# Rows of log decays from a table and one product per tile, and the gates ahead of the features, in a hybrid DeltaNet and attention step

## Chip, cores and metric

One core of a Trainium2 chip. The metric is the device time of one execution in microseconds. TensorE multiplies matrices (PE in the profile, its weight loads PEld), VectorE (DVE), ScalarE (ACT) and GpSimd (POOL) work on elements, SyncE (SP) issues all DMAs of this kernel. [...]

## What is computed

Two layers with a width of 1024, over 512 latent and 128 context tokens (640 columns). Each layer has a modulated norm, one input projection for three mixers, their gated sum, and an MLP with squared ReLU. Mixer A, the one that matters here, is a gated DeltaNet with 8 heads of 64, in both directions, in chunks of 64 tokens:

```python
beta = sigmoid(beta_raw)                      # per token, direction, head
g = -exp(a_log) * softplus(alpha_raw + dt_bias)
gc = cumsum(g_, axis=-1)                      # within a chunk of 64 tokens
diff = gc[..., :, None] - gc[..., None, :]
decay = where(incl, exp(where(incl, diff, 0.0)), 0.0)
a_mat = where(strict, b_[..., :, None] * kk * decay, 0.0) + eye(CHUNK)
sol = triangular_solve(a_mat, rhs, lower=True, unit_diagonal=True)
attn = einsum('nbhid,nbhjd->nbhij', q_, k_) * decay
```

The 64x64 matrix `decay` of each chunk, head and direction needs the log decays gc once along its rows and once along its columns. Mixer B is global attention, mixer C attention in a window.

## The kernel before

All large products have operands split in two float32r parts (a rounded part and the rest), three matmuls for each piece of 128 input channels, over halves of 320 columns.

In each layer the norm writes the operands `hh` and `hl`. Then comes the DeltaNet stretch. `gdn_feat(hp, sk)` (L384 to L407) computes for a pair of heads the projections of keys, queries and values (tag mb), the short convolution of five steps on VectorE (L400 to L402) and SiLU. It runs for the first pair at L435. After that, L437 to L511 compute the gates of all tokens and heads: a load of the 32 columns `w_ba`, a product with `hh` and `hl` (L448), a chain of some twenty small VectorE and ScalarE steps to log beta (`lnb`) and `g` (L481), products with triangles of ones that sum g within chunks (L487, L488), and the column terms `c3` (L495, L496), kept per partition.

`gdn_prep(hp, t, ...)` prepares a tile of 128 tokens (two chunks) for two heads: transposes, norms of keys and queries (`tm`, `kq`), then the rows of log decays. For these, GpSimd multiplies g with the triangle `t64` (L553) and log beta with the identity (L554), VectorE subtracts (L555), and TensorE multiplies the result `rm` with blocks of ones (`onesc`, L558), so that each partition gets the sums of its chunk along the columns. A second product with the identity, in bf16, adds the mask `mskb` (zero or -1e30, L559). VectorE subtracts the column terms (L562), ScalarE takes the exponential (L563), and the result `ee` multiplies the products of keys with keys and queries (L568 to L581).

`gdn_solve` inverts the 32x32 blocks of five tiles on VectorE (L588 to L601), `gdn_post` and `gdn_scan` finish the pair. `weave` lets the steps for pair hp go beside features, preparation and solve of pair hp + 1; `pipe` keeps two tiles in flight. Attention follows (`att_front`, `att_back`), its preparation beside the last pair.

Fillers: `unit(u)` (L409) computes 36 projections that are needed later and writes them to DRAM (`f_spill`); in layer 0 products for the modulation (L252) stand between them. `branch(0)` and `branch(1)` follow in the same way. These have a priority that lies below all else, and tag fm. Their products are paced (`pace`, L194): each group of four waits for an empty instruction on SyncE, which waits for a group eight products back.

The order of each engine's instructions is fixed when the program is built, by a list scheduler that takes the program's order as priority and simulates the engines. Each engine and SyncE run their list in order.

Of the kernel before, what the change touches and what calls it, by code (L numbers as in the profile page):

```python
# [17 lines left out]
P = 128  # L18
DM = 1024
NT = 640  # L20
# [50 lines left out]
def weave(*gens):  # L71
    active = list(gens)
    while active:
        live = False
        for g in list(active):
            try:
                live |= next(g) is None
            except StopIteration:
                active.remove(g)
        if not live:  # L80
            return
# [11 lines left out]
def kernel(ctx: ExitStack, tc: tile.TileContext, d: dict):  # L93
# [185 lines left out]
    def norm(l, n, half, x, hh, hl, sc, ks=range(KC)):  # L279
# [34 lines left out]
        yield  # L314

    x_spill = dp.tile([P, KC, NT], F32, name="x_spill")
    a_spill = dp.tile([4, P, NT], F32, name="a_spill")
# [19 lines left out]
    for l in range(DEPTH):  # L337
# [35 lines left out]
        def gtile(shape, tag, dt=F32):  # L373
            return (gp if tag in G_EARLY else gdl).tile(shape, dt, name=tag, tag=tag, bufs=GB.get(tag, 1))
# [58 lines left out]

        sk = gtile([P, 3, 642], "sk")
        weave(gdn_feat(0, sk))  # L435

        ba = gtile([P, 5, 32], "ba")  # L437
# [57 lines left out]
        tt(out=c3[:, 0:2], in0=gc, in1=lnb, op=SUB)  # L495
        ts(out=c3[:, 2], in0=gc[:, 1], scalar1=-1.0, scalar2=None, op0=MUL)  # L496
        kbe = gtile([P, 2, 5, 8], "kbe")
        tt(out=kbe.rearrange("p d t h -> p d (t h)"), in0=pgc[:, 1],
# [12 lines left out]
        ACT.activation(egs.rearrange("p c t h -> p c (t h)"), gs, AF.Exp)  # L511

        cnt, busy, dbusy = [0, 0], {}, {}

        def gdn_prep(hp, t, sk, stg, out):
# [34 lines left out]
            ACT.copy(kq, pkq)  # L550
            rm = gtile([P, 3, 2, 64], "rm")
            lb = gtile([P, 2, 64], "rlb")
            ptt(out=rm[:, 0:2], in0=bc(g[:, :, t, h2], 3, 64), in1=bc(t64, 2, 2), op=MUL)  # L553
            ptt(out=lb, in0=bc(lnb[:, 1, t, h2], 2, 64), in1=bc(i64, 1, 2), op=MUL)  # L554
            tt(out=rm[:, 2], in0=lb, in1=rm[:, 1], op=SUB)  # L555
            yield
            pgr = bank([P, 3, 2, 64], "mb")
            PE.matmul(pgr, lhsT=onesc, rhs=rm, start=True, stop=False)  # L558
            PE.matmul(pgr, lhsT=identb, rhs=bc(mskb, 2, 2), start=False, stop=True)  # L559
            yield  # L560
# [773 lines left out]
def _pack(w):  # L1334
    a = np.ascontiguousarray
    w = {k: np.asarray(v) for k, v in w.items()}
    o = {}
    o["cst"], o["msk"], o["rope"] = _consts()
    xs = np.concatenate([w["x_sample"][0], w["x_prompt"][0]], 0)
    o["xT"] = a(xs.T.reshape(KC, P, NT).transpose(1, 0, 2))  # L1340
# [56 lines left out]
```

## Time and profile before

| | us |
|---|---|
| median of 3 runs | 2795.83 |
| lowest and highest run | 2795.57, 2800.28 |
| the profiled execution, whole | 2802.05 |
| its span, first to last instruction | 2800.3 |
| TensorE busy (95% of the span) | 2667.8 |
| VectorE busy | 1972.1 |
| ScalarE busy | 1210.0 |
| GpSimd busy | 963.0 |

The mean granted clock of TensorE is 0.98. Matmuls overlap in time: the duration of a row is longer than the time after which the next one starts. What a product costs is therefore read from start to start. Busy shares are means over stages with different limits.

### The profile page before, as it was taken

How to read it: one execution, taken by the hardware profiler on the slowest of the kernel's cores; microseconds unless marked ns; L12 is line 12 of the kernel's file. 1: busy time of each engine (PE TensorE's matmuls, PEld its weight loads, DVE VectorE, ACT ScalarE, POOL GpSimd, SP SyncE). 2: the span in 40 equal slices, each digit the busy share in tenths (PEclk: the TensorE clock that was granted, in tenths of full speed). 3: DMA queues.
4: the chain of work that ended last, by engine and by line, in shares of the span. 5: the costliest groups of instructions: out<-in, count | busy, mean ns of one | idle time of the engine just before them, and what ended most of it. 6: DMA issues, size and time to landing. Idle time of an engine off the chain costs nothing. (4 is left out here: it accounts for less than half of the span.)

```text
span 2800.3 us, 55175 instructions
## 1 busy us (share of the span) xinstructions
PE 2667.8 (95%) x20868; PEld 2447.0 (87%) x20868; DVE 1972.1 (70%) x4315; ACT 1210.0 (43%) x2846; POOL 963.0 (34%) x1259
## 2 busy tenths in 40 slices
PE   6989999999999999999999899899999899999999
PEld 4887787788978999999988888788998789999999
DVE  4687797555567678999966887965556676676664
ACT  3434435445544442444344345344455453343342
POOL 2434434454445211122125444344554630111120
PEclk8999999999999999999999999999999999999999
DMA  7222212333234423455422211112223242222231
GB/s 252 88 77 72 85 35 72 115 115 95 81 100 137 144 80 110 147 156 154 149 88 77 82 48 59 39 49 91 94 80 111 77 145 76 69 84 76 68 98 61
DMA packets 117145, 268.61 MB, mean 96 GB/s; under 512 B 13712, under 2 KB 22544, under 8 KB 116880
## 3 DMA queue, kind: packets, MB, share of 16 engines
q1 hardware_dynamic: 116880, 265.08, 29.2%
q8 instruction: 166, 2.72, 0.4%
q14 instruction: 99, 0.81, 0.1%
HBM read 232.52 MB, written 32.51 MB: 95 GB/s over the span
## 5 line engine op out<-in xcount | busy, mean ns | idle before, releaser
L419 PE MATMUL fm<-hh,fhi 128*128 128x320 f32 x2304 | 448.6, 326 | 6.5 <-ACT hh L311 2.9
L419 PEld LDWEIGHTS fm<-hh,fhi 128*128 128x128 f32 x2304 | 360.8, 195 | 23.6 <-issue 7.5
L165 POOL TENSOR_TENSOR rl<-fr,rh 128x320 fp32r<-128x320 f32 x128 | 144.3, 1133 | 673.3 <-ACT rh L164 669.3
L165 POOL TENSOR_TENSOR flo<-fraw,fhi 128x512 fp32r<-128x512 f32 x176 | 237.1, 1348 | 298.3 <-ACT fhi L164 191.4
L164 ACT CAST ghi<-graw 128x1024 fp32r<-128x1024 f32 (+1 forms) x148 | 145.0, 980 | 224.8 <-PE gm L1251 128.9
L419 PE MATMUL fm<-hh,flo 128*128 128x320 f32 x1152 | 238.7, 327 | 2.6 <-SPq L198 2.6
L1100 DVE SCALAR_TENSOR_TENSOR x<-gm,mod,x 128x320 f32<-128x320 f32 (+2 forms) x384 | 154.0, 432 | 85.4 <-PE gm L1251 84.7
L1251 PE MATMUL gm<-rh,ghi 128*128 128x320 f32 x1024 | 195.5, 310 | 3.5 <-DVE x L1100 3.4
L165 DVE TENSOR_TENSOR glo<-graw,ghi 128x1024 fp32r<-128x1024 f32 (+1 forms) x148 | 171.8, 1161 | 35.3 <-ACT ghi L164 20.3
L1251 PE MATMUL gm<-rl,ghi 128*128 128x320 f32 x1024 | 196.6, 310 | 0.0
L419 PEld LDWEIGHTS fm<-hh,flo 128*128 128x128 f32 x1152 | 183.0, 195 | 10.5 <-issue 4.1
L1251 PE MATMUL gm<-rh,glo 128*128 128x320 f32 x1024 | 192.0, 309 | 0.0
L164 ACT CAST fhi<-fraw 128x512 fp32r<-128x512 f32 x192 | 118.8, 619 | 157.8 <-PE fm L419 80.5
L186 PE MATMUL mb<-hh,whi 128*128 128x320 f32 x1024 | 167.6, 312 | 4.8 <-ACT whi L164 4.8
L1251 PEld LDWEIGHTS gm<-rh,ghi 128*128 128x128 f32 x1024 | 160.9, 188 | 5.9 <-DVE x L1100 2.8
L1251 PEld LDWEIGHTS gm<-rl,ghi 128*128 128x128 f32 x1024 | 161.7, 188 | 1.0 <-issue 1.0
L1251 PEld LDWEIGHTS gm<-rh,glo 128*128 128x128 f32 x1024 | 160.8, 188 | 0.0
L186 PEld LDWEIGHTS mb<-hh,whi 128*128 128x128 f32 x1024 | 152.4, 188 | 9.0 <-ACT whi L164 6.3
L267 DVE SCALAR_TENSOR_TENSOR macc<-fraw,csil,macc 128x512 f32<-128x512 f32 x168 | 135.1, 822 | 0.0
L1189 PE MATMUL gm<-hh,ghi 128*128 128x320 f32 x768 | 130.2, 310 | 0.0
L963 DVE TENSOR_REDUCE mx<-s 128x1 f32<-128x640 f32 (+3 forms) x160 | 99.9, 632 | 37.4 <-PE s L953 23.0
L595 DVE TENSOR_TENSOR sv<-sv,stmp 128x31 f32<-128x31 f32 (+15 forms) x248 | 121.3, 489 | 5.8
(324 smaller groups left out, 6217.8 us busy)
## 6 DMA issues: line engine op xcount, KB each, us to landing
graw<-w_ff SPq DMA_DIRECT2D x128, 512.0 KB, 3.4
fraw<-w_mod SPq DMA_DIRECT2D x160, 256.0 KB, 2.8
fraw<-w_fm SPq DMA_DIRECT2D x144, 256.0 KB, 2.8
f_spill<-fgt SPq DMA_DIRECT2D x72, 320.0 KB, 2.2
wraw<-w_fm SPq DMA_DIRECT2D x32, 512.0 KB, 3.3
gts<-f_spill SPq DMA_DIRECT2D x48, 320.0 KB, 3.2
fraw<-w_br SPq DMA_DIRECT2D x48, 256.0 KB, 2.8
graw<-w_o SPq DMA_DIRECT2D x20, 512.0 KB, 4.5
```

Source lines behind the costliest of these rows:

```text
L164: ACT.copy(hi, src)
L165: (lo_eng or DVE).tensor_tensor(out=lo, in0=src, in1=hi.bitcast(F32), op=SUB)
L186: mm = PE.matmul(ps, lhsT=w_[k], rhs=x_[:, k, s], start=(i == 0 and k == 0), stop=(i == 2 and k == n - 1))
L267: stt(out=a, in0=raw, scalar=c, in1=a, op0=MUL, op1=ADD)
L419: mm = PE.matmul(ps[half], lhsT=w[:, k], rhs=x_[:, 4 * q + k, s], start=(q == 0 and k == 0 and w is hi and x_ is hh), stop=(q == 1 and k = ...
L595: tt(out=XX[:, s + 1:32, 0:m], in0=XX[:, s + 1:32, 0:m], in1=tv, op=SUB)
L963: DVE.tensor_reduce(out=mx, in_=pv, axis=AX.XY if n > 512 else AX.X, op=ALU.max)
L1100: stt(out=x[:, j, a:b], in0=ps[:, a - t0:b - t0], scalar=gate[:, j, c:c + 1], in1=x[:, j, a:b], op0=MUL, op1=ADD)
L1189: PE.matmul(ps, lhsT=w_[:, 4 * q + k], rhs=x_[o][:, k], start=(first and i == 0 and k == 0), stop=(i == 2 and k == 3), skip_group_check=True)
L1251: PE.matmul(ps, lhsT=w_[k], rhs=r[k // 2][o][:, k % 2, half_of(half)], start=(i == 0 and k == 0), stop=(i == 2 and k == 3))
```

## The change

The gates are computed before the features of the first pair. From the sums within chunks a table is made once a layer: for all tiles the forward sums, the backward sums, and log beta less the backward sums, 24 columns per token (`g3`). TensorE transposes it to rows, which are split into a float32r part and the rest (`ghi`, `glo`), written to DRAM (`g_spill`), and read back with ten small DMAs so that partition 4t + 2i + c holds the rows of part i, chunk c of tile t. Partitions 64 to 127 of the result `grow` hold the mask. A selector `rsel`, loaded once a layer, has for each tile ones that pick the four partitions of the tile, and an identity that picks the mask. In `gdn_prep` one float32r product of `rsel[:, t]` and `grow` gives the sum of rows and mask.

```diff
+    g_spill = dp.tile([2, 24, NT], F32, name="g_spill")
...
-        sk = gtile([P, 3, 642], "sk")
-        weave(gdn_feat(0, sk))
...
+        g3 = gtile([P, 5, 3, 8], "g3")
+        DVE.tensor_copy(g3[:, :, 0:2].rearrange("p t d h -> p d t h"), gc)
+        tt(out=g3[:, :, 2], in0=lnb[:, 1], in1=gc[:, 1], op=SUB)
+        prow = bank([P, 4, P], "ma"), bank([P, P], "ma")
+        for t in range(5):
+            PE.transpose(prow[0][0:24, t] if t < 4 else prow[1][0:24], g3[:, t].rearrange("p k h -> p (k h)"), ident)
+        ghi, glo = (gtile([P, NT], "zz", F32R) for _ in range(2))
+        for a, b, ps in ((0, NL, prow[0].rearrange("p t i -> p (t i)")), (NL, NT, prow[1])):
+            ACT.copy(ghi[0:24, a:b], ps[0:24])
+            tt(out=glo[0:24, a:b], in0=ps[0:24], in1=ghi[0:24, a:b].bitcast(F32), op=SUB)
+        rst = gtile([P, 24, 64], "rst")
+        rsel = gtile([P, 5, P], "rsel", F32R)
+        nc.sync.dma_start(out=rst.rearrange("p r i -> p (r i)")[:, 0:NT], in_=d["sel"])
+        ACT.copy(rsel.rearrange("p t i -> p (t i)"), rst.rearrange("p r i -> p (r i)")[:, 0:NT])
+        rst = gtile([P, 24, 64], "rst")
+        POOL.memset(rst[0:64], 0.0)
+        for i, part in enumerate((ghi, glo)):
+            nc.sync.dma_start(out=g_spill[i], in_=part[0:24].bitcast(F32))
+            for t in range(5):
+                nc.sync.dma_start(out=rst[4 * t + 2 * i:4 * t + 2 * i + 2],
+                                  in_=g_spill[i, :, t * P:t * P + P].rearrange("r (c j) -> c r j", c=2))
+        grow = gtile([P, 3, 8, 64], "grow", F32R)
+        ACT.copy(grow[0:64].rearrange("p k g i -> p (k g) i"), rst[0:64])
+        DVE.tensor_copy(grow[64:128], bc(mskb[64:128], 2, 8))
...
+        sk = gtile([P, 3, 642], "sk")
+        weave(gdn_feat(0, sk))
...
-            rm = gtile([P, 3, 2, 64], "rm")
-            lb = gtile([P, 2, 64], "rlb")
-            ptt(out=rm[:, 0:2], in0=bc(g[:, :, t, h2], 3, 64), in1=bc(t64, 2, 2), op=MUL)
-            ptt(out=lb, in0=bc(lnb[:, 1, t, h2], 2, 64), in1=bc(i64, 1, 2), op=MUL)
-            tt(out=rm[:, 2], in0=lb, in1=rm[:, 1], op=SUB)
-            yield
             pgr = bank([P, 3, 2, 64], "mb")
-            PE.matmul(pgr, lhsT=onesc, rhs=rm, start=True, stop=False)
-            PE.matmul(pgr, lhsT=identb, rhs=bc(mskb, 2, 2), start=False, stop=True)
+            PE.matmul(pgr, lhsT=rsel[:, t], rhs=grow[:, :, h2], start=True, stop=True)
```

## Rows read from the trace of the kernel before

**Rows 1.** The page: busy time of each engine, share of the span, instructions.

```profile
PE 2667.8 (95%) x20868; PEld 2447.0 (87%) x20868; DVE 1972.1 (70%) x4315; ACT 1210.0 (43%) x2846; POOL 963.0 (34%) x1259
```

**Rows 2.** Timeline of TensorE, ends of attention: start, us, engine, line, operation, tiles.

```profile
896.38 0.44 PE L1010 MATMUL pt<-ph,VT 128*64 128x128 f32 x4 [0.61 <-DVE ph L1005]
...
901.86 0.75 PE L186 MATMUL fm<-yhl,fhi 128*128 128x320 f32 x4
...
2223.74 0.75 PE L186 MATMUL fm<-yhl,flo 128*128 128x320 f32 x4
...
2266.46 0.44 PE L1010 MATMUL pt<-ph,VT 128*64 128x128 f32 x4 [0.61 <-ACT yhl L164]
```

**Rows 3.** Two windows: length, busy time of PE, PEld, DVE, ACT, POOL; clock, DMA.

```profile
110.00:120.00 10.00, 8.34 (x41) 7.77 (x40) 6.21 (x17) 2.48 (x9) 6.11 (x9) 0.66 0.26 80
...
2230.00:2240.00 10.00, 7.31 (x55) 4.59 (x54) 8.91 (x27) 6.85 (x22) 3.02 (x4) 1.00 0.01 2
```

**Rows 4.** Timeline of TensorE around one decay product, and two filler groups.

```profile
148.87 0.38 PE L543 MATMUL mb<-cst,tm 128*128 128x128 f32 x2
149.08 0.81 PE L558 MATMUL mb<-rm,cst 128*128 128x384 f32 x2
149.73 0.33 PE L559 MATMUL mb<-mskb,identb 128*128 128x384 bf16 x1
149.76 0.88 PE L419 MATMUL fm<-hh,flo 128*128 128x320 f32 x4
150.48 0.75 PE L419 MATMUL fm<-hh,fhi 128*128 128x320 f32 x4
...
185.69 1.34 PE L419 MATMUL fm<-hh,fhi 128*128 128x320 f32 x8
186.87 0.82 PE L419 MATMUL fm<-hh,flo 128*128 128x320 f32 x4
```

**Rows 5.** Lines 553 to 555: count, ns min/median/max, first and last start.

```profile
L553 POOL TENSOR_TENSOR rm<-g,cst x40: 608/617/687, 113.6 to 1852.1; 128x256 f32<-128x256 f32 x40
...
L554 POOL TENSOR_TENSOR rlb<-lnb,cst x40: 391/401/444, 112.8 to 1834.0; 128x128 f32<-128x128 f32 x40
...
L555 DVE TENSOR_TENSOR rm<-rlb,rm x40: 278/291/1347, 118.9 to 1852.7; 128x128 f32<-128x128 f32 x40
```

**Rows 6.** Timelines of DVE and POOL: one solve step without and with L553.

```profile
158.08 0.28 DVE L595 TENSOR_TENSOR sv<-sv,stmp 128x112 f32<-128x112 f32 x1
...
199.87 0.57 DVE L595 TENSOR_TENSOR sv<-sv,stmp 128x112 f32<-128x112 f32 x1
...
199.62 0.69 POOL L553 TENSOR_TENSOR rm<-g,cst 128x256 f32<-128x256 f32 x1 [0.59 <-PE mb L558]
```

**Rows 7.** Timeline of all engines, start of layer 1 up to the first decay product.

```profile
1463.32 0.99 PE L419 MATMUL fm<-hh,fhi 128*128 128x320 f32 x5 [0.22 <-ACT hh L311]
...
1465.77 1.05 ACT L164 CAST whi<-wraw 128x1024 fp32r<-128x1024 f32 x1 [0.40 <-DMA wraw<-w_fm]
...
1491.80 4.84 PE L448 MATMUL mb<-hh,whi 128*64 128x320 f32 x32
...
1496.80 0.83 DVE L406 SCALAR_TENSOR_TENSOR sk<-so,sk 128x642 f32<-128x642 f32 x1 [0.81 <-ACT so L206]
...
1509.80 0.37 ACT L550 COPY kq<-mb 128x256 f32<-128x256 f32 x1
...
1512.15 0.30 DVE L481 SCALAR_TENSOR_TENSOR g<-rm,ealog 128x40 f32<-128x40 f32 x2
...
1514.58 0.24 DVE L493 COPY gc<-ma 128x80 f32<-128x80 f32 x1 [0.21 <-PE ma L488]
...
1516.10 0.81 PE L558 MATMUL mb<-rm,cst 128*128 128x384 f32 x2
```

**Rows 8.** DMA issues (KB, us to landing), and SyncE's waits from 60 to 600 us (total, times, longest).

```profile
f_spill<-fgt SPq DMA_DIRECT2D x72, 320.0 KB, 2.2
...
SPq L198 <- PE fm L419: 339.0, 234, 11.9
```

More of the change, by code (lines that the diff above doesn't have):

```diff
@@ L1338, in _pack @@
     o["cst"], o["msk"], o["rope"] = _consts()
+    sel = np.zeros((P, 5, P), np.float32)
+    for t in range(5):
+        for r in range(4):
+            sel[4 * t + r, t, 64 * (r % 2):64 * (r % 2) + 64] = 1
+    sel[64:] = (np.arange(P) % 64 == np.arange(64)[:, None])[:, None]
+    o["sel"] = sel.reshape(P, NT)
     xs = np.concatenate([w["x_sample"][0], w["x_prompt"][0]], 0)
```

## Prediction

> **What bounds the kernel now.** I read the page first: TensorE is busy in 95% of the span, VectorE in 70%, GpSimd in 34% [rows 1]. A mean says nothing about one stage, so I then asked which work ends each layer's stretch of DeltaNet and attention, the only stretch that the change touches. The filler products (tile fm: `unit`, then `branch(0)` and `branch(1)`) have the lowest priority and are there to take TensorE's gaps. In layer 0 they still run at 901.86, five microseconds after the last attention product at 896.38: up to that point TensorE always had something to do, so its total work sets the end. In layer 1, which has no modulation units among its fillers, the last filler product starts at 2223.74 and attention goes on to 2266.46 [rows 2]: there the chain of DeltaNet and attention steps sets the end, and TensorE runs at 7.31 of 10 us behind the last filler [rows 3]. So the two layers ask two questions: how much TensorE work goes away (layer 0), and how much of it stood on the chain (layer 1).
>
> **The products of `gdn_prep`.** Each of the 40 calls (4 head pairs, 5 tiles, 2 layers) issues at L558 an fp32 product, which the trace shows as two matmuls of 128x384, and at L559 a bf16 product that adds the mask. Start to start in one such place: the pair begins at 149.08, the mask product at 149.73, four filler matmuls follow, and the next group begins at 150.48. That is 1.40 us. Four filler matmuls of 320 columns take 0.59 us (eight in 1.18, from 185.69 to 186.87). So pair and mask hold TensorE for 0.81 us [rows 4]. The single product that takes their place is in the type of the filler products (float32r), 384 columns: 0.147 us x 384/320 = 0.18 us. I take this value, not its ends: it cannot stream faster than the bf16 product of the same width (about 0.16 us, what 0.81 less 0.65 leaves), and at worst it holds the engine for the 0.33 us that the bf16 row lists as its whole duration. The saving is 0.63 us a call, 25.2 us in all (19 to 26).
>
> What of that reaches the end: in layer 0, 20 x 0.63 = 12.6 us of a sum that TensorE sets, taken whole; it is replaced by nothing, since fillers move up into it. In layer 1 the slot stands in the chain of each tile, but two tiles go side by side and fillers stand in the same queue, so between none and all of 12.6 us comes through; I take 10. The five small transposes per layer that build the table cost ten slots like those at L543, two of which fill the 0.21 us from 148.87 to 149.08 [rows 4]: 1 us in all. **Together -21.6 us.**
>
> **The vector work of `gdn_prep`.** L553 and L554 go from GpSimd (40 x 0.617 and 40 x 0.401 us, 41 us), L555 from VectorE (40 x 0.291, 11.6 us) [rows 5]. GpSimd has slack and the removal there would be worth nothing by itself. VectorE gets back work that stood between the features and the product; most of it ran while VectorE had to wait for the product anyway. One more effect is in the rows: a solve step of 128x112 takes 0.28 us at 158.08 and 0.57 us at 199.87, when a GpSimd product of L553 has run since 199.62 [rows 6]. So a meeting costs VectorE 0.29 us, and at most one for each of 40 calls, 11.6 us; how many of them meet a step that is late I don't know. Between 0 and 12, I take -2 us, near the lower end, because L553 mostly runs while VectorE waits for TensorE.
>
> [...]
>
> **Gates ahead of the features.** In layer 1 the operands are ready at 1463.32. The gates' product (L448) starts only at 1491.80, behind the features' products, and ends at 1496.64 (4.84 more); the features end on VectorE at 1497.63 (1496.80 + 0.83); the gates' vector chain gives g at 1512.45 (1512.15 + 0.30). The keys of the first tile stand ready at 1510.17 (1509.80 + 0.37), and yet its decay product starts at 1516.10 [rows 7]: the wait for the gates is 6 us. With the gates first, their product can take the slot at 1463.32 that fillers have, so the features slip little; but VectorE must then do the gate chain (16 us from the end of L448 to g) and the new table work between the features' steps. So the first decay product comes between 6 us earlier and no earlier. I take -3 us in layer 1. [...] **Together -3 us.**
>
> **The table, and what it queues.** Once a layer: a copy and a subtraction of 120 columns, two splits of 640, a cast of 64x1536 on ScalarE and one on VectorE, a cast of 640 and a memset of 64x1536. The nearest row is the cast of 128x1024 in 1.05 us [rows 7]; by columns the two large casts are 1.6 us each and the sum 5 to 7 us a layer over three engines, hidden by the features' products as long as these last (28 us from the operands to L448); uncovered they belong to the start above. Its 13 DMAs are issued by SyncE: one load of the selector, two writes to DRAM, ten small reads that each wait for a write. A comparable write lands after 2.2 us [rows 8], a read in about that, so writing and reading back take 5 to 6 us, and table plus round trip about 14 us behind the gates. From 1463.32 on that is 23 us of gates (1491.80 to 1514.58 and the copy there) and 14, about 1500, before the 1510 at which the keys are ready [rows 7]. What stands behind a waiting read in SyncE's queue are the loads of the next weights and the steps that pace the fillers (L198), and a filler product waits for that step. One stall of 2 to 3 us in each round trip, with 8 products of slack (1.2 us): between 0 and 6 us a layer, and only where the chain has nothing to give TensorE. I take 1.5 us each. **Together +3 us.**
>
> **Sum.** -21.6 - 2 - 3 + 3 = -23.6 us. The profiled execution took 2802.05 us (span 2800.3 and 1.75 around it), so it would take 2778.4. The median of the runs, 2795.83, is 0.22% below that execution; with the same difference: **2772 us**.
>
> **Rivals.**
> [...]
> (b) *The slots are saved and stay empty.* The chain runs on VectorE's steps in the solves and the fillers are limited by their own loads and splits, so shorter products become longer waits. Only some 5 us of layer 0 come through: 2791. For it: TensorE already has gaps in both stretches of [rows 3]. Against: in layer 0 the fillers outlast everything. That the product isn't a single pass would end here too; the filler rows in the same type speak against it.
> (c) *Slower: the table is late.* SyncE issues in order, and its queue spends 339 us of the first stretch waiting in pace steps, once for 11.9 us [rows 8]. If the ten reads are spread between such steps, 3 us each, the table comes 30 us later than I reckon, at about 1530: the first decay product of layer 1 is 14 us later than now, all of it at the end. In layer 0 fillers are drawn forward in that wait and missing later; say the same 14. Price: 28 us against 20.6 saved (the start's gain is gone): 2803. It decides from about 13 us a layer later than now on (2 x 13 less 20.6 is the 5.6 us below). Against it: the scheduler can put reads ahead of loads that aren't urgent.
>
> **How the numbers follow.** The forecast 0.62, (a) 0.15, (b) 0.14, (c) 0.09. A difference of 0.2% (5.6 us) is about what a measurement of this kernel can tell from no change: faster is below 2790.2, slower above 2801.4. The forecast with its bounds (2760 to 2785) and (a) lie in faster, (b) lies at its edge, in the same. That gives 0.77, 0.14, 0.09. The range goes from 2753, a little below (a), to 2793, which takes in (b), and leaves out (c) and the far ends.
>
> **What would show each step.** One product of 128x384 per call, about 0.2 us from its start to the next, and TensorE's busy time lower by 25 to 35 us (the rows' durations overlap, so this is more than the slots). The gates' product before the features' products; the first decay product of layer 1 within 47 to 53 us of the operands. The last fillers of layer 0 still about level with the end of attention; layer 1's attention ending 10 to 16 us sooner counted from its operands. GpSimd's busy time lower by 38 us. Rows in which fillers wait for SyncE no longer than now. I am wrong if the first decay product waits for the cast of the table, if layer 1 doesn't shorten although its product does, or if TensorE's idle time grows by what the products lose.

## Result and the profile after

The changed kernel takes 2811.62 us (median; 2809.65 to 2815.69) against 2795.7 us of the kernel before, run beside it: 1.0052 times as long, with a 95% interval from 1.0038 to 1.0066. It is **0.5% slower**; forecast were 0.8% less, and the time lies outside the range and on its other side.

The page's row of busy times, for [rows 1]. TensorE has lost 70 matmuls but only 3 us, where 25 to 35 were expected; GpSimd is 35 us lower, VectorE no lower.

```profile
PE 2664.8 (95%) x20798; PEld 2445.8 (87%) x20798; DVE 1976.0 (70%) x4285; ACT 1212.5 (43%) x2854; POOL 927.7 (33%) x1181
```

The new product in the timeline (start, duration, engine, line, operation), for [rows 4]. It holds TensorE for 0.26 and 0.18 us from its start to the next group's, where pair and mask held it for 0.81. Over the 38 of 40 calls that run at a granted clock of 1.00 with no wait behind them the median is 0.26 us, so a call saves some 0.55 us where 0.63 was forecast. The part of the change that was to save time does so.

```profile
1530.67 0.42 PE L577 MATMUL mb<-grow,rsel 128*128 128x384 f32 x1
1530.93 0.74 PE L420 MATMUL fm<-hh,flo 128*128 128x320 f32 x4
1531.51 0.34 PE L577 MATMUL mb<-grow,rsel 128*128 128x384 f32 x1
1531.69 0.89 PE L420 MATMUL fm<-hh,fhi 128*128 128x320 f32 x5
```

The start of layer 1 in the timeline, for [rows 7]; the operands are ready at 1475.82, and brackets hold a wait and what ended it. The table is not late: all ten reads are issued in one go at 1509.90, the cast of what they bring ends at 1517.39, and the first decay product, 1530.67, is 13 us behind it. The features are late. The gates' weights take the buffer `whi`, so the cast of the first feature weights waits until the gates' product ends (1484.20), GpSimd's split waits for that, and the features' first product starts 11.7 us behind the operands (3.5 before); the features end at 1522.81, 47 us behind them (34 before). How much of these 13 us the buffer makes, e7_wba asks below.

```profile
1479.83 4.37 PE L446 MATMUL mb<-hh,whi 128*64 128x320 f32 x29
1484.56 1.05 ACT L164 CAST whi<-wraw 128x1024 fp32r<-128x1024 f32 x1
1485.68 2.36 POOL L165 TENSOR_TENSOR wlo<-wraw,whi 128x1024 fp32r<-128x1024 f32 x1 [7.20 <-ACT whi L164]
1487.53 4.27 PE L186 MATMUL mb<-hh,whi 128*128 128x320 f32 x28
1509.90 3.54 SPq L515 DMA_DIRECT2D rst<-g_spill  x10
1515.91 1.48 ACT L518 CAST grow<-rst 64x1536 fp32r<-64x1536 f32 x1
1521.98 0.83 DVE L407 SCALAR_TENSOR_TENSOR sk<-so,sk 128x642 f32<-128x642 f32 x1 [0.81 <-ACT so L206]
```

The ends in the timeline, for [rows 2]: last filler product and last attention product of layer 0, then of layer 1. In layer 0 the fillers now outlast attention by 14 us instead of 5, and both are later than before although TensorE has less to do.

```profile
914.16 0.75 PE L186 MATMUL fm<-yhl,flo 128*128 128x320 f32 x4
900.01 0.44 PE L1028 MATMUL pt<-ph,VT 128*64 128x128 f32 x4 [0.61 <-DVE ph L1023]
2236.48 0.80 PE L186 MATMUL fm<-yhl,flo 128*128 128x320 f32 x4
2275.60 0.44 PE L1028 MATMUL pt<-ph,VT 128*64 128x128 f32 x4 [0.61 <-ACT yhl L164]
```

**Where the time went.** Busy time hides it, because it counts a matmul longer where the granted clock (the profile gives it as a share of the full one) is lower: a product of L713 took 0.14 us at 538.25, at 0.50, and the same product in the kernel before (L695 there) 0.07 us at 536.54, at 1.00 (rows below). So I cut each layer's stretch of DeltaNet and attention (in layer 0 from the start of the span, in layer 1 from the operands, to the first addition to the residual) into windows of 2 us and add up three things: work, which is TensorE's busy time times its granted clock; lost, busy time times what the clock lacks of 1; and idle. The whole stretches as windows (window, length, busy us and rows of PE, PEld, DVE, ACT and POOL, granted clock, DMA share, GB/s), before:

```profile
0.00:940.30 940.30, 871.68 (x7456) 755.07 (x7457) 621.57 (x1477) 416.78 (x1077) 406.11 (x567) 0.97 0.33 106
1463.70:2308.50 844.80, 802.65 (x6611) 712.19 (x6610) 588.42 (x1382) 392.71 (x1018) 397.01 (x536) 0.99 0.25 81
```

and after:

```profile
0.00:951.40 951.40, 873.01 (x7422) 756.59 (x7423) 624.63 (x1463) 417.35 (x1081) 388.98 (x528) 0.95 0.33 105
1475.80:2318.20 842.40, 798.57 (x6576) 709.87 (x6575) 586.14 (x1367) 393.71 (x1022) 377.85 (x496) 0.98 0.25 81
```

By the 2-us windows, both stretches together: work 1638 us before and 1615 after, **23 less**; idle 111 and 122, **11 more**; lost to the clock 36 and 56, **20 more**. The sum is the 9 us by which these two profiled executions differ there; outside the stretches they differ by 1 us. The medians differ by 16 us: the profiled execution before was the longest of its four.

Two places hold most of the loss. In layer 0 TensorE waits 2.04 us at 523.76 for attention's read of `f_spill`, and what stands behind it are narrow products: 64x64 ones and the modulation's 128x32. Eight products of L713 take 1.12 us there:

```profile
523.76 0.44 PE L899 MATMUL pt<-cst,fr 128*128 128x128 f32 x2 [2.04 <-DMA fr<-f_spill]
524.04 0.81 PE L663 MATMUL ma<-r,dbd 128*128 128x128 f32 x4
538.25 1.12 PE L713 MATMUL ma<-abd,Y 128*64 128x128 f32 x8
```

In the kernel before the same read ends a wait of 1.30 us, and sixteen of the same products of 128x128 take 1.09 us, half as long each:

```profile
521.52 0.44 PE L881 MATMUL pt<-cst,fr 128*128 128x128 f32 x2 [1.30 <-DMA fr<-f_spill]
536.54 1.09 PE L695 MATMUL ma<-abd,Y 128*64 128x128 f32 x16
```

In layer 1 it waits 3.01 us at 2161.31 for a split of `q_prep`; the last filler product ahead of it ends at 2158.3:

```profile
2157.85 0.46 PE L186 MATMUL fm<-yhl,fhi 128*128 128x320 f32 x2
2161.31 1.08 PE L945 MATMUL pt<-identr,kst 128*128 128x128 f32 x8 [3.01 <-DVE kst L165]
```

The windows round both places: behind each wait TensorE is busy at a mean granted clock of 0.53 for 18 and 22 us, and it returns to 1.00. In windows of 1 us the clock is 0.50, the lower clock in what follows, from 525 to 541 and from 2163 to 2183; only the first and the last window of each stretch lie between (0.65 and 0.82, 0.85 and 0.91). These two cost 8.5 and 9.7 us of the clock.

```profile
515.00:524.00 9.00, 5.61 (x61) 4.18 (x60) 3.88 (x8) 4.72 (x16) 6.89 (x22) 1.00 0.74 231
524.00:542.00 18.00, 18.00 (x147) 10.32 (x146) 6.44 (x17) 6.58 (x26) 3.69 (x5) 0.53 0.25 79
542.00:560.00 18.00, 18.00 (x186) 15.64 (x186) 7.29 (x21) 9.72 (x28) 12.13 (x20) 1.00 0.38 125
2150.00:2162.00 12.00, 8.99 (x73) 8.18 (x72) 7.61 (x14) 3.40 (x11) 10.89 (x11) 1.00 0.31 89
2162.00:2184.00 22.00, 20.73 (x99) 15.49 (x99) 11.64 (x34) 11.24 (x33) 4.01 (x4) 0.53 0.05 19
2184.00:2200.00 16.00, 16.00 (x118) 13.64 (x117) 11.68 (x28) 7.68 (x20) 13.24 (x17) 1.00 0.14 38
```

In the kernel before the same two places run at 1.00, and the second has no wait; behind its first 62 us its longest time at the lower clock in these stretches is 10 us and costs 4.4.

```profile
518.00:536.00 18.00, 16.70 (x196) 12.67 (x194) 8.19 (x23) 8.70 (x30) 7.69 (x20) 1.00 0.56 177
2147.92 1.01 PE L927 MATMUL pt<-identr,kst 128*128 128x128 f32 x8
2120.00:2180.00 60.00, 58.99 (x463) 53.48 (x463) 42.05 (x98) 31.21 (x77) 32.69 (x36) 1.00 0.36 108
```

### The profile page after: what moved, and what is told of

Read it like the earlier page. It is cut to its first block, busy times and chain, and to the rows that moved or that the text cites. A ratio compares the mean times of both kernels' runs of the same rounds, so it can differ in the third digit from the quotient of the medians.

```text
span 2810.0 us, 54997 instructions
## 1 busy us (share of the span) xinstructions
PE 2664.8 (95%) x20798; PEld 2445.8 (87%) x20798; DVE 1976.0 (70%) x4285; ACT 1212.5 (43%) x2854; POOL 927.7 (33%) x1181
## 5 line engine op out<-in xcount | busy, mean ns | idle before, releaser
L420 PE MATMUL fm<-hh,flo 128*128 128x320 f32 x1152 | 236.7, 325 | 2.6 <-SPq L198 2.4
L989 ACT ACTIVATE p<-s,nb 128x640 f32<-128x640 f32 (+3 forms) x160 | 103.0, 648 | 52.2 <-PE pt L1019 31.4
```

The source lines that it names most:

```text
L420: mm = PE.matmul(ps[half], lhsT=w[:, k], rhs=x_[:, 4 * q + k, s], start=(q == 0 and k == 0 and w is hi and x_ is hh), stop=(q == 1 and k = ...
L989: ACT.activation(pw, pv, AF.Exp, bias=nb[:, h:h + 1], scale=0.125, accum_out=den[:, h:h + 1])
```

## The experiments

Four theories. **T**: the build of the table costs it. **B** and **W**: the gates ahead of the features cost it, W by the shared buffer. **R**: a shorter product is given back as a longer wait behind it, always. **O**: the order in which the engines' instructions stand, which a list scheduler works out anew for each build, puts waits where TensorE has nothing to fill them with. (The first four expectations below call O theory A, and T theory C.) All results in one table: the kind of product (the pair with the mask, or the one that takes its place), times as a ratio to the kernel before, run on the same chip, with the 95% interval; work, idle and lost in us as above, and the number of waits of TensorE of 2 us or more in these stretches (from 62 us on), from one profiled execution each. The last columns scatter: n1_swap, whose TensorE order is that of before, has 4 us less idle and 6 less lost, and e13_wba_held, in the order of e2_gates_first, 10 more lost. A second measure of the clock needs no profile: each run's span times what its mean granted clock lacks of 1, averaged over the kernel's runs. It is 50 us for the kernel before (a run lies some 5 us off the mean), 48 for e2_gates_first, 51 for e13_wba_held, 53 for e11_change_held, but 68 for the changed kernel, 70 for e12_old_in_new_order and 77 for e1_table_only.

Where the text says how many rows stand at another place, TensorE's rows in two traces are compared in order of time, by line and tiles, without the decay products and the table's transposes: 20,748 rows.

| kernel | products | order of issue | ratio | work | idle | lost | waits |
|---|---|---|---|---|---|---|---|
| before | pair | own | 1 | 1638 | 111 | 36 | 7 |
| n1_swap | pair | TensorE's as before | 0.9996 (0.9985 to 1.0006) | 1637 | 107 | 30 | 7 |
| e2_gates_first | pair | own | 1.0010 (1.0000 to 1.0020) | 1640 | 109 | 27 | 7 |
| e6_table_unused | pair | own | 1.0030 (1.0019 to 1.0041) | 1640 | 117 | 35 | 7 |
| e8_wba_before | pair | own | 1.0038 (1.0024 to 1.0052) | 1637 | 118 | 38 | 9 |
| e9_wba_gates | pair | own | 1.0095 (1.0078 to 1.0111) | 1642 | 128 | 39 | 12 |
| e13_wba_held | pair | that of e2 | 1.0020 (1.0005 to 1.0034) | 1638 | 111 | 37 | 7 |
| e12_old_in_new_order | pair | that of the changed kernel | 1.0125 (1.0103 to 1.0146) | 1640 | 121 | 53 | 14 |
| e3_one_pass | pair, one pass | own | 0.9994 (0.9983 to 1.0005) | 1618 | 115 | 46 | 9 |
| e10_one_pass_held | pair, one pass | that of before | 0.9971 (0.9959 to 0.9982) | 1621 | 116 | 35 | 9 |
| the changed kernel | one | own | 1.0052 (1.0038 to 1.0066) | 1615 | 122 | 56 | 17 |
| n2_after_kq | one | own | 1.0002 (0.9990 to 1.0015) | 1614 | 127 | 45 | 14 |
| e1_table_only | one | own | 1.0095 (1.0080 to 1.0111) | 1620 | 131 | 55 | 15 |
| e4_no_table | one | own | 1.0018 (1.0005 to 1.0031) | 1613 | 123 | 48 | 12 |
| e5_ms5 | one | own | 1.0029 (1.0017 to 1.0041) | 1608 | 131 | 49 | 12 |
| e7_wba | one | own | 0.9963 (0.9951 to 0.9976) | 1615 | 122 | 31 | 9 |
| n3_e7_kq | one | own | 0.9973 (0.9962 to 0.9984) | 1618 | 116 | 39 | 9 |
| e11_change_held | one | that of e2 | 0.9947 (0.9929 to 0.9965) | 1619 | 119 | 27 | 10 |
| e14_change_wba_held | one | that of e2 | 0.9955 (0.9943 to 0.9967) | 1616 | 123 | 27 | 10 |
| e16_no_table_held | one | that of e2 | 0.9955 (0.9940 to 0.9970) | 1613 | 119 | 39 | 10 |

### The parts of the change one by one

**e1_table_only**, the changed kernel with the features ahead of the gates again:

```diff
+        sk = gtile([P, 3, 642], "sk")
+        weave(gdn_feat(0, sk))
         ba = gtile([P, 5, 32], "ba")
...
-        sk = gtile([P, 3, 642], "sk")
-        weave(gdn_feat(0, sk))
         cnt, busy, dbusy = [0, 0], {}, {}
```

> The changed kernel with the features issued ahead of the gates again: the table and the one product per tile stay, the move of the gates is undone. Theory A (order): the saving of the product is real in each tile, and what ate it are new waits of 2 to 3 us behind which TensorE's granted clock is at its lower level for some 20 us, wherever the new order happens to put them. Then this kernel has its own such places, neither the old nor the new ones; the time lies between 2775 and 2810, and the clock lost (time times one less the granted clock; 56 us before, 77 after) differs from both and moves with the time. Theory B (the move costs it): the features, 10 to 13 us later than before in each layer, are the loss; undone, the time is 2773 to 2780, the features end some 34 us behind layer 1's operands as they did, and DeltaNet of layer 0 ends earlier than before by 10 us. Theory C (the table costs it): near 2811, as the changed kernel.

Measured: 2824.18 us, 0.95% slower, outside every theory's figure. Undoing the move does not give the 30 us that B had for it, but it does not price the move either, since the table is late here and the order new. The table is late as rival (c) had it, though not through reads spread in SyncE's queue: the gates stand behind the features (their product at 1511.41), and the first decay product waits for the cast of the table, 67 us behind layer 1's operands (52 before), and in layer 0 at 130.40 (120.8 before):

```profile
128.88 1.47 ACT L521 CAST grow<-rst 64x1536 fp32r<-64x1536 f32 x1 [6.90 <-DMA rst<-g_spill]
130.40 1.01 PE L578 MATMUL mb<-grow,rsel 128*128 128x384 f32 x2 [0.17 <-ACT grow L521]
```

**e2_gates_first**, the kernel before with `weave(gdn_feat(0, sk))` behind the gates:

> The kernel before with the features issued behind the gates, the diagonal blocks and the mask product kept: the move alone. Theory B: slower than before by 20 to 35 us, 2816 to 2830, since nothing is saved in the products, with the features of layer 1 ending some 47 us behind the operands as in the changed kernel. Theory A: anywhere from 2790 to 2815, with the features as late as that but the time going with the clock lost. Theory C: no slower than before by more than 5 us.

Measured: 2798.24 us, 0.1% above before, with the features ending at 1503, 47 us behind the operands, as in the changed kernel. The late features cost next to nothing, and B, which had 20 to 35 us for them, is out. The order has hardly moved either: 653 rows stand at another place than before.

**e3_one_pass**, the kernel before with blocks and ones in float32r:

```diff
-            rm = gtile([P, 3, 2, 64], "rm")
+            rm = gtile([P, 3, 2, 64], "rm", F32R)
...
-            PE.matmul(pgr, lhsT=onesc, rhs=rm, start=True, stop=False)
+            PE.matmul(pgr, lhsT=onesr, rhs=rm, start=True, stop=False)
```

`onesr` is a copy of the ones in float32r, made once at the start.

> The kernel before with the product of the diagonal blocks made in one pass: blocks and ones in float32r. It leaves out the low part of each log decay (they are rounded to what one pass takes); the blocks, the mask product and the place of the features stay. It takes one of the two fp32 passes away, about 0.4 of the 0.63 us a call that the table saves, 40 times: 16 us of TensorE's slots, with no table, no new wait and no move. By the sum of the prediction: 2782 to 2787. Theory A: the saving shows in the place itself (pair to next group 0.3 to 0.4 us shorter), but the time lies anywhere from 2780 to 2805 because the order behind it changes. Theory B and C: 2782 to 2787, as the prediction's sum has it.

Measured: 2794.14 us, no change (-0.06%), though work falls by 21 us. Neither table nor move is in this kernel, and the saving still does not reach the end; only O had a range that takes this in. In its build 8,225 rows stand at another place, though on TensorE nothing but the length of one product has changed.

**n1_swap**, two statements exchanged that issue on GpSimd (L553 and L554):

> The kernel before with its two GpSimd products of the diagonal blocks (L553 and L554) issued in the other order: the same instructions, nothing saved or added. It measures what a reordering by itself does. Theory A: a time that differs from the one before by 3 to 12 us, to either side, with the clock lost changed by about as much. Theories B and C: the same time, within 3 us.

Measured: 2792.69 us, the same. It was meant as a reordering, but the build left TensorE's order as it was: 2 rows stand at another place. So it is a control: same order, same time.

**e6_table_unused**, e2_gates_first with the build of the table added, and nothing that reads it:

> The kernel with the gates ahead and the old products (e2_gates_first, 2798) and the build of the table added, whose result nothing reads. It prices the build alone. Theory T: 2813 to 2830. Theory O: 2797 to 2802, the build hidden beside the features. By the prediction's terms for transposes and queue: 2802.

Measured: 2808.95 us, between the ranges of T and O: 0.2% above e2_gates_first, twice the term of the prediction (1.5 us a layer), with idle and lost up by 8 each and 1,676 rows at another place. **e4_no_table**, the changed kernel without the build:

> The changed kernel without the build of the table: no transposes, no split, no writes to DRAM, no reads back; grow and rsel are filled with constants on VectorE and ScalarE, so the decays are not those of the gates. The one product per tile and the gates ahead of the features stay. Theory T (the build of the table and what it queues costs 15 to 30 us): 2780 to 2792, the table's cost gone and a part of the products' saving left. Theory O (the one product itself leads to an order of the instructions with new waits and a lower granted clock): 2805 to 2815, as the changed kernel, with the clock lost between 500 and 550 us (10 us in the changed kernel, none before) still there. By the prediction's sum for products, vector work and start: 2769.

Measured: 2803.32 us, again between the two ranges: 0.18% above before and so some 10 us under the changed kernel, but far from the 2769 of the sum. T is at best a quarter of the 40 us between forecast and result. The 10 us lost at 500 to 550, which O had expected to stay, shrink to 3. With 5,367 rows at another place than in the changed kernel, this run prices a new order along with the table.

### Does a reordering alone move the time?

**e5_ms5**, the changed kernel with `MS, MP = 5, 1`, a modulation unit behind every fifth filler:

> The changed kernel with a modulation unit behind every fifth filler unit instead of every fourth. Same instructions, other places of the narrow 128x32 products. Theory O: the stretch at 524 to 542, where these products stand around a wait of 2 us for f_spill, keeps the higher clock, and some 8 us come back: 2800 to 2805. Theory T: within 4 us of 2811, whatever the clock does there.

Measured: 2808.88 us, 0.23% less than the changed kernel (ratio to ratio). By its time the run lies within T's 4 us of 2811, by its ratio, 6.5 us under the changed kernel, where O had it: it decides nothing. The place does what O said, the clock at 524 to 542 is 1.00 again. But 5 us are lost at 750 to 762 instead, and idle time grows by 9: losses come up at other places. Its work is some 7 us lower than that of its like; why stays open.

**n2_after_kq**, the changed kernel with two ScalarE copies issued in the other order:

```diff
+            ACT.copy(kq, pkq)
             for h in range(2):
                 o = slice(64 * h, 64 * h + 64)
                 ACT.copy(kz[o, h], pkq[o, 0])
-            ACT.copy(kq, pkq)
```

> The changed kernel with ScalarE's copy of kq put ahead of the two half copies into kz: the same instructions in another order of issue. Theory O: a time that differs from the changed kernel's by 0.2 to 0.6%, with the clock lost (63 us in the two DeltaNet and attention stretches) changed by about as many us as the time. Theory W or T (the cause is fixed to a resource): within 0.15% of the changed kernel, 0.37 to 0.67% above before.

Measured: 2799.87 us, 0.5% less than the changed kernel, with 12 us less lost to the clock: the same instructions, 3,411 rows at another place. This is what O had forecast, and it speaks against a cause that is tied to one resource. **n3_e7_kq** is the same edit in e7_wba:

> The same reordering of ScalarE's copies in e7_wba. Theory W: within 0.15% of e7_wba, that is 0.2 to 0.5% below before. Theory O: anywhere between e7_wba and the changed kernel, 0.4% below to 0.5% above before.

Measured: 2791.66 us, 0.1% above e7_wba and 0.27% below before, inside the spans of both theories: it decides nothing.

**e7_wba**, the changed kernel with a buffer of its own for the gates' weights:

```diff
-        wba = gtile([P, KC, 2, 32], "whi", F32R)
+        wba = gtile([P, KC, 2, 32], "wba", F32R)
```

The name is added to the early buffers (`G_EARLY`) as well.

> The changed kernel with a buffer of its own for the gates' split weights (wba), which there shares the buffer whi with the first feature weights, so that the cast of these waits for the gates' product (1484.2 in layer 1). Expected of every theory: the first features' product starts some 4 us behind layer 1's operands instead of 12, the features end 6 to 8 us earlier. If the late features cost time, 2798 to 2805; if what bounds the first tiles is the gates' chain on VectorE, 2808 to 2814.

Measured: 2789.41 us, 0.37% faster than before and 0.9% less than the changed kernel, far more than expected. And the reason that I gave is not in it: the features' first product does start 8.3 us behind the operands instead of 11.7, but the features end 46 us behind them, 1 us earlier: VectorE works through the gates' chain from 1473.5 on and begins the convolution at 1481.7, although ScalarE's first step of it stands ready at 1478.98.

```profile
1473.51 0.20 DVE L455 TENSOR_SCALAR ee<-ba 128x80 f32<-128x80 f32 x1 [9.95 <-ACT ba L452]
1478.15 0.83 ACT L401 ACTIVATE sk<-cb,conv 128x642 f32<-128x642 f32 x1
1481.73 0.88 DVE L403 SCALAR_TENSOR_TENSOR sk<-cb,conv,sk 128x642 f32<-128x642 f32 x1
```

The gain goes with 26 us less lost to the clock in the profiles.

**e9_wba_gates** and **e8_wba_before** put the same buffer into e2_gates_first and into the kernel before:

> The old products with the gates ahead of the features and a buffer of its own for the gates' weights: e7_wba without the table and the one product. Theory W (the shared buffer is the loss: whoever frees it gains, whatever the products): as far below e2_gates_first (0.1% above before) as e7_wba is below the changed kernel (0.9%), so 0.7 to 0.9% below before, 2770 to 2776. Theory O (order: each build puts the waits and the stretches at the lower clock elsewhere, and e7_wba drew a good order): within 0.3% of before. In both the stretches without waits keep about 842 us of layer 0 and 791 of layer 1 as work at the full clock, where the changed kernel has 827 and 782.

> The kernel before with a buffer of its own for the gates' weights, everything else kept, the features ahead of the gates. The gates' product no longer waits until the third feature weight is cast. Theory W: 0.2 to 0.5% faster. Theory O: within 0.3% of before, to either side.

Measured: 2827.15 and 2811.54 us, 0.95% and 0.38% *slower*. The buffer is no gain where W had 0.2 to 0.9%; W is out. O's ranges, within 0.3% of before, were missed as well, by e9_wba_gates three times over: it had taken the effect of an order for smaller than it is. With the same instructions as e2_gates_first and 5,240 rows at another place, e9_wba_gates has 19 us more idle time, 12 us more lost, and 12 long waits instead of 7.

### The order held

What was open now: does the order do it, or do shorter products lengthen the waits whatever the order? The builder takes edges between two instructions of one engine that fix their order and wait for nothing. With them one kernel can be built in another's order, on all five engines; in outline:

```python
for engine, order in held.items():        # places in the other kernel's build
    q = [i for i in instructions if i.engine == engine]
    for a, b in zip(order, order[1:]):
        tc.add_manual_dep(q[b], q[a].name, NO_SYNC)
```

Instructions that only one of the two kernels has stay free; the one product takes the place of the first of the pair. The traces bear it out: of 20,748 rows at most 68 stand at another place than in the kernel whose order is held, against 9,535 between e2_gates_first and the changed kernel.

**e13_wba_held**: e9_wba_gates in the order of e2_gates_first.

> e9_wba_gates (old products, gates ahead, a buffer of its own for the gates' weights; 0.95% above before) held in the order of e2_gates_first, which has the same instructions. Theory O: 0.0 to 0.2% above before, the time of e2_gates_first. If the buffer itself (its place, its waits) is the cost: 0.7 to 1.0% above before.

Measured: 2803.82 us; 0.75% of the 0.95% are gone, with 7 long waits again. The order made e9_wba_gates slow, not its buffer. Nor do the edges cost much: 0.1% against e2_gates_first, within the intervals.

**e12_old_in_new_order**: the old products in the order of the changed kernel.

> The reverse: e2_gates_first, old products and no table, held in the order of the changed kernel; the mask products and the instructions that make the diagonal blocks are placed freely. Theory O: the order brings its losses along and the old products cost their 20 to 25 us more: 1.0 to 1.5% above before, 2825 to 2840. Theory R: 0 to 0.4% above before.

Measured: 2830.67 us, 1.25% slower and 1.15% above e2_gates_first, which has the same instructions, as O had it. In the profiles 26 us more are lost to the clock and 12 more idle; by the clocks of all runs 21 us of some 32 are the clock. The place in layer 1 comes back with products that have nothing to do with the change: the same wait in the timeline,

```profile
2182.04 1.08 PE L926 MATMUL pt<-identr,kst 128*128 128x128 f32 x8 [2.98 <-DVE kst L165]
```

and the same 22 us at 0.53 in the windows:

```profile
2170.00:2182.00 12.00, 9.06 (x73) 8.22 (x71) 7.36 (x14) 3.52 (x10) 11.61 (x11) 1.00 0.30 94
2182.00:2204.00 22.00, 20.66 (x98) 15.57 (x99) 11.18 (x33) 11.07 (x32) 4.00 (x4) 0.53 0.08 26
```

The place in layer 0 does not come back; the rest of the 53 us lost lies elsewhere.

**e11_change_held**: the changed kernel, complete, in the order of e2_gates_first.

> The changed kernel with its instructions held in the order of e2_gates_first (the old products with the gates ahead, 0.1% above before); only the table's own instructions are placed freely, and the one product stands where the pair stood. Nothing is left out. Theory O: the prediction's sum comes through against that kernel: 0.6 to 0.9% below before, 2772 to 2782. Theory R: 0.0 to 0.3% above before. Theory T (the build of the table costs 6 us a run, as e6_table_unused suggests) takes 0.2% of the gain away in either.

Measured: **2783.73 us, 0.53% faster than before** and 1% under the changed kernel; 0.6% under e2_gates_first, whose order it has. That is a little outside O's range and far from R's. In the timeline the eight products of the second place start without a wait,

```profile
2129.28 1.00 PE L945 MATMUL pt<-identr,kst 128*128 128x128 f32 x8
```

the windows round them and over the whole stretches show the higher clock (the last two lines are the stretches of e2_gates_first):

```profile
2120.00:2200.00 80.00, 74.23 (x553) 65.41 (x549) 47.83 (x108) 35.03 (x88) 49.69 (x50) 1.00 0.32 97
0.00:926.90 926.90, 856.13 (x7421) 747.29 (x7422) 622.81 (x1462) 418.23 (x1081) 388.94 (x528) 0.98 0.33 108
1451.90:2290.60 838.70, 790.46 (x6576) 706.78 (x6575) 582.64 (x1366) 393.43 (x1021) 376.46 (x495) 0.99 0.25 82
0.00:932.60 932.60, 865.25 (x7456) 748.15 (x7457) 624.30 (x1478) 416.51 (x1077) 408.53 (x567) 0.98 0.32 107
1456.00:2299.10 843.10, 801.65 (x6611) 710.79 (x6610) 596.61 (x1383) 393.13 (x1018) 399.07 (x541) 0.99 0.24 81
```

Against e2_gates_first: work 20 us less, lost the same, idle 10 us more in these two profiles; that of e2_gates_first was the shortest of its 12 runs, and by the ratios 17.6 us arrive. R as it stands, always and whole, is out; a part of the saving is given back. **e10_one_pass_held**, e3_one_pass in the order of before:

> e3_one_pass with all five engines' instructions held in the order of the kernel before by edges that order and do not wait; the product in one pass is then the only difference (and the low part of the log decays is left out, as there). Theory O (the order takes the saving): idle and clock losses stay near those of before, so the time falls by the products' 20 us: 2774 to 2782, 0.6 to 0.8% faster. Theory R (a shorter product is given back as a longer wait behind it, in any order): within 0.2% of before, as e3_one_pass was.

Measured: 2789.12 us, between the two theories: by the ratio 8 us come through of the 18 by which work falls.

**e16_no_table_held** and **e14_change_wba_held** take e11_change_held apart: without the build of the table, and with a buffer of its own for the gates' weights.

> e4_no_table (one product per tile, constants in place of the table, so the decays are not those of the gates) held in the order of e2_gates_first, as e11_change_held is. Theory T (the table's build takes the missing third): 2775 to 2779, 0.6 to 0.8% below before. Theory R (the third is given back as waits behind the shorter products): within 0.15% of e11_change_held, 0.4 to 0.65% below before.

> e11_change_held with a buffer of its own for the gates' weights. If the shared buffer costs something by itself: 0.1 to 0.3% faster than e11_change_held, 2776 to 2781. If only the order counted in e7_wba: within 0.15% of e11_change_held, 2780 to 2788.

Measured: 2784.24 and 2783.51 us, both within 0.1% of e11_change_held. In a fixed order neither the table's build nor the shared buffer costs anything that can be measured. What is missing of the sum shows as idle time: 119 to 123 us in these three kernels, 109 and 111 in the two with the pair in the same order. Behind which waits it stands is not shown.

## Why the prediction was wrong

**The step that failed** is the sum itself, where it says that in layer 0 the products' 12.6 us count whole, "since fillers move up into it", and that 10 of 12.6 come through in layer 1. The premise, that up to the last attention product of layer 0 TensorE "always had something to do", does not hold in the trace it was read from: between 62 and 896 us it was idle for 40 us. And the sum took these idle times (111 us in both stretches) and the 36 us lost to the clock as standing still. But the order of issue is made when the program is built, from simulated durations (`schedule_with_timeline_sim=True` in the kernel), and a product that is shorter there, or a block of statements that is moved, can give another order throughout (8,225 of 20,748 rows in e3_one_pass). With the same instructions, orders differ by 0.75% (e9_wba_gates and e13_wba_held) and by 1.15% (e12_old_in_new_order and e2_gates_first); the second is more than the whole forecast. The change happened to get a poor one: its order costs the old products those 1.15%, and the order of e2_gates_first gives its own products 1% back (e11_change_held).

**Products: right.** Forecast 21.6 us less of TensorE with the transposes; work falls by 23 from before to after, by 25 in the changed kernel's order, by 20 in the order of e2_gates_first. A call's product takes 0.26 us where 0.18 was taken, inside the bounds; the shortest of the 40 takes 0.17.

**What reaches the end: too much even in a held order.** Of the forecast's 23.6 us there arrive, by the ratios, 14.8 against before (0.53% of 2796) and 17.6 against e2_gates_first; in the two profiles idle time takes back 10 of the 20 us of work, in e10_one_pass_held 10 of 18 are missing by the ratio. So rival (b), slots that are saved and stay empty, was right in part, and I gave it 0.14 as a case of its own where it is a share of every held case.

**Vector work.** GpSimd is 35 us lower where 38 were said; VectorE's busy time went from 1972.1 to 1976.0. The 11.6 us for L555 were its median times 40; its rows add up to 14.8. In the solve, where the -2 was to come from, nothing came back: its 496 steps of the kind in [rows 6] take 236.7 us in e2_gates_first and 239.4 in e11_change_held, in the same order and without L553 and L554. They take 239.3 us in the kernel before and 235.5 in the changed kernel, in different orders.

**Gates ahead.** -3 us were forecast, with features that "slip little". They slip by 13 us. The buffer `whi`, which I had not looked up in the code, makes about 1 us of that (46 us in e7_wba, which has its own); the rows of e7_wba show VectorE in the gates' chain when the convolution could start, which the prediction named and priced too low. The first decay product comes 55 us behind the operands, where 47 to 53 were said and 52 before. It costs less than it looks: 0.1% in e2_gates_first, whose features are as late. No run shows a time near that of (a), which has a chance of 0.15 and sets the range's lower end of 2753: the shortest median of any kernel here is 2783.51 us (e14_change_wba_held).

**The table.** +3 us forecast; 0.2% in e6_table_unused, nothing in a held order. Rival (c) named the right side for a wrong reason: the reads are not spread, and the table is ready 13 us early. It is late only where the gates stand behind the features, in e1_table_only, which is what moving them ahead is good for.

**The signs I named.** The one that came true was the last: idle time grew, from 132.5 to 145.2 us over the span, and with it the time at the lower clock, which I had not listed. Another came near: layer 1's attention ends only 3 us sooner counted from its operands, where 10 to 16 were said. TensorE's busy time was no sign at all, because of the 23 us that the products gave, the clock took 20.

What stays open: why one order loses more than another is shown at two places only; whether the builder's simulation could be led to better ones was not tried. Nor is it shown that the order of e2_gates_first is a good one rather than a fair one.

## What to carry to other kernels

Where a list scheduler makes the order at build time, a small edit is two edits: the one in the text and a new order. Before a gain or loss of under one per cent is put down to the edit, hold the order and change only the work, or hold the work and change the order, and count work, idle time and time at the lower clock separately, since busy time mixes them. If the edit saves work, build it in the order that was already good: here that turned +0.5% into -0.5%.

## What the hardware showed that was not expected

A wait of TensorE can be followed by a loss of several times its length. Behind the waits of 2.04 and 3.01 us the granted clock was 0.53 for 18 and 22 us in which the engine was busy nearly all the time, with narrow products and attention's steps behind it, and 8.5 and 9.7 us were lost: with the wait itself 11 and 13 us. In the kernel before, TensorE waited 1.30 us at 521.52, at the first of these places, for the same read; wide filler products stood round it (128x320, at 522.16 and 523.19), and the clock stayed at 1.00. Nor is the length of the wait the price: one of 3.52 us in the kernel before, with fillers close behind it, was followed by 22 us at 0.93.

```profile
1693.31 0.33 PE L716 MATMUL ma<-H,wm 64*64 64x64 f32 x2 [3.52 <-DVE H L720]
1694.00:1716.00 22.00, 22.00 (x184) 20.26 (x182) 15.51 (x27) 11.05 (x28) 12.60 (x28) 0.93 0.25 88
```

What makes the difference is not shown by these few places. Over both stretches the time at the lower clock cost between 27 and 56 us among kernels, a spread as large as what the change was to save.
